# All of w_down's columns by Strassen's algorithm in groups 0 to 6 of a two-layer encoder, with results added on GpSimd

## The chip, the cores and the metric

The kernel runs on one core of one Trainium2 chip. The metric is the device time of one execution in microseconds (us). A core has TensorE (PE, matrix multiply; PEld is its weight load), VectorE (DVE), ScalarE (ACT) and GpSimd (POOL), which run side by side from queues in program order, and SyncE (SP), which issues most transfers. SBUF is the on-chip memory, PSUM the eight banks into which TensorE writes.

## The reference, cut to what matters

Two layers of a bidirectional encoder on 256 tokens of width 2048. The change lies in the last two lines of a layer:

```python
for l in range(DEPTH):
    ...
    x = x + jnp.einsum('bse,ed->bsd', mix, w_o[l])
    h = rmsnorm(x, norm_mlp[l])
    u = jax.nn.relu(jnp.einsum('bsd,df->bsf', h, w_up[l]))
    x = x + jnp.einsum('bsf,fd->bsd', u * u, w_down[l])
return rmsnorm(x, norm_final)
```

Here w_up is 2048 x 8192 and w_down 8192 x 2048, all in 32-bit floats.

## The kernel before, in words

**Steps.** All weight products are cut into steps, one per 128x1024 block of weights (512 KB), kept in one list (`Step`, L465). For each step the program, written out by the loop at the end, does three things ahead of its matmuls: `load` (L964) issues the transfer seven steps ahead on SP's queue; `split` (L978) cuts the weights into a high part `whi` (a cast on ScalarE, L988) and a low part `wlo` (a subtraction on VectorE, L989), two or three steps ahead, into three buffers each; and `prep`, where a step has one, runs five steps ahead. A product is then the sum of high x high, high x low and low x high, so a weight block costs one ScalarE and one VectorE instruction of 1024 columns besides its matmuls.

**The MLP.** The 8192 hidden columns are cut into eight groups of 1024. `up_steps(g)` (L657) has 16 steps, four for each block `q` of 256 hidden columns; the block is evacuated by ScalarE and VectorE (L668 to L676: sum, rectify and scale, square, split). Its result `uT[q]` has a high and a low part. For the Strassen products `sums_of` (L707) forms the four sums S1 to S4 of the left factor (L712 to L714) and splits them (L716, L717). Group g + 1's w_up steps are mixed with group g's w_down steps by the list `order` (L846).

**w_down.** Before, columns 1024 to 2047 of a group are plain steps (`down_steps`, 8 steps of 12 matmuls through `mode_b`, L477), and columns 0 to 1023 are one 2 x 2 Strassen product in Winograd's form (`strassen_steps`, L761): seven products P1 to P7, two steps each (one per half `h` of the rows), six matmuls per step (L802) instead of the plain form's eight products. The right factors are sums of weight blocks, formed by VectorE (L815, L817, L821, L832) in place or into `t2`. Three PSUM banks (`a`, `d`, `b`) carry the products, `a` and `d` accumulating over several of them. After each product its bank is added to or subtracted from x by VectorE (L782, PSUM and SBUF in, SBUF out). Group 7 is plain.

**Buffers.** Raw weights land in `wraw` (five), or for Strassen in `spare0`, `spare1` (B11, one per row half) and `side` (four: B12, B22, B21). `mid` has six buffers of 512 columns, `big` has 24, and the matmul banks are six besides the pair of `score_banks`.

Of the kernel before, what the change touches and what calls it, by code (L numbers as in the profile page):

```python
# [23 lines left out]
P = 128  # L24
# [19 lines left out]
def tile_trunk(ctx: ExitStack, tc: tile.TileContext, x_in, w_in, w_o, w_up, w_down,  # L44
# [459 lines left out]
    def layer_steps(l):  # L504
# [152 lines left out]
        def up_steps(g):  # L657

            out_, evacs = [], []
            for q in range(4 * g, 4 * g + 4):  # L660
                box = {}

                def evac(q=q, box=box):
                    need(("rrow", l))
                    a = mid(F32, 2, 256)
                    for i in range(2):

                        nc.scalar.copy(a[:, i, :], box["b"][i][:, 256:512])  # L668
                        nc.vector.tensor_add(a[:, i, :], a[:, i, :], box["b"][i][:, 0:256])
                    nc.vector.scalar_tensor_tensor(  # L670
                        a, a, 0.0, rrow.rearrange("p (o c) -> p o c", o=1).to_broadcast([P, 2, 256]),
                        op0=ALU.max, op1=ALU.mult)
                    nc.scalar.activation(a, a, AF.Square, bias=zero1[:, 0:1])
                    u = big(F32R, 2, 2, 256)
                    nc.scalar.copy(u[:, 0], a)
                    nc.vector.tensor_sub(u[:, 1], a, f(u[:, 0]))  # L676
                    uT[q] = u
                    if q < 28:
                        sums_of(q, a)
# [27 lines left out]
        def sums_of(q, a):  # L707
# [3 lines left out]
            a11, a21, a12 = v[:, 0, :], v[:, 1, :], v[:, 2, :]  # L711
            nc.vector.tensor_sub(sm[:, 0:2, :], v[:, 0:4:3, :], v[:, 1:2, :].to_broadcast([P, 2, P]))  # L712
            nc.vector.scalar_tensor_tensor(sm[:, 2, :], sm[:, 1, :], -1.0, a11, op0=ALU.mult, op1=ALU.subtract)
# [6 lines left out]
        def down_steps(g, js):  # L720
            out_ = []
            for j in js:
                box = {}
                for k in range(4):
                    def mm(wh, wl, j=j, k=k, box=box):
                        if k == 0:
# [3 lines left out]
                        hts = [uT[4 * g + k]] * 2  # L730
                        mode_b(box["b"], hts, wh, wl, [0, 1], k == 0, k == 3, blocks=(0,) if final else (0, 1),
                               lo_last=g < 7)
# [7 lines left out]
                        if final:  # L740
# [3 lines left out]
                            for c in range(2):  # L744
                                cols = slice(c * 256, c * 256 + 256)
                                for i, (hts, vh, vl) in enumerate(box["w"]):
                                    mode_b([None, tail[c]], hts, vh[:, :, cols], vl[:, :, cols], [0, 1],
# [10 lines left out]
                    out_.append(Step(w_down[l, (g * 4 + j) * 4 + k], 2, 512, None, mm, fourth=g == 7))  # L758
            return out_

        def strassen_steps(g):  # L761
# [5 lines left out]
            raw, t2, box = {}, {}, {}  # L767

            def src(par, j, h):
                return w_down[l, g * 16 + (par * 2 + j) * 2 + h]  # L770

            def left(name, q):

                if name[0] == "A":
                    t, kk = int(name[1]) - 1, int(name[2]) - 1
                    return [uT[q][:, i, kk, t * P:(t + 1) * P] for i in range(2)]
                return [sT[q][:, i, "3124".index(name[1]), :] for i in range(2)]

            def evac(bank, t, j, sign):
                xs = x[:, t, j * 512:(j + 1) * 512]  # L780
                op = nc.vector.tensor_add if sign > 0 else nc.vector.tensor_sub
                op(xs, xs, bank)  # L782


            plan = [("P1", "A11", "a", True, (0, 0, 1)), ("P6", "S2", "a", False, (1, 0, 1)),
                    ("P7", "S3", "d", True, (1, 1, -1)), ("P5", "S1", "a", False, (1, 1, -1)),
                    ("P3", "S4", "a", False, (0, 1, -1)), ("P2", "A12", "b", True, (0, 0, 1)),
                    ("P4", "A22", "d", False, (1, 0, 1))]
            out_ = []
            for name, lf, bk, fresh, dst in plan:  # L790
                for h in range(2):
# [19 lines left out]
                    elif name == "P6":  # L811
                        loads = [(("B12", h), src(0, 1, h), None), (("B22", h), src(1, 1, h), None)]

                        def prep(h=h):
                            nc.vector.tensor_add(raw["B11", h], raw["B11", h], raw["B12", h])  # L815
                            t2[h] = big(F32, 2, 512)
                            nc.vector.tensor_add(t2[h], raw["B22", h], raw["B11", h])  # L817
                        get = lambda h=h: t2[h]
                    elif name == "P7":
                        def prep(h=h):  # L820
                            nc.vector.tensor_add(raw["B12", h], raw["B12", h], raw["B22", h])  # L821
                        get = lambda h=h: raw["B12", h]
# [4 lines left out]
                    elif name == "P2":  # L827
                        loads = [(("B21", h), src(1, 0, h), None)]
                        get = lambda h=h: raw["B21", h]
                    else:  # L830
                        def prep(h=h):
                            nc.vector.tensor_add(t2[h], raw["B21", h], t2[h])  # L832
                        get = lambda h=h: t2[h]
                    stp = Step(None, 2, 512, None, mm, fourth=False, prep=prep, raw=get,
# [5 lines left out]
        for g in range(7):  # L840
            ss = down_steps(g, (2, 3)) + up_steps(g + 1)
            hs = strassen_steps(g)

            order = [0, 0]
            for p_ in range(7):
                order += [1, 0, 1] + ([0, 0] + [0] * (p_ in (1, 3, 5)) if p_ < 6 else [])  # L846
            assert order.count(0) == len(ss) and order.count(1) == len(hs), (order.count(0), order.count(1))
            steps.extend(hs.pop(0) if o else ss.pop(0) for o in order)
        steps.extend(down_steps(7, range(4)))
# [258 lines left out]
def _pack_down(w, g):  # L1108

    plain = [_pack(w[:, j * 512:(j + 1) * 512], 2) for j in range(4)]  # L1110
    if g < 7:
        b = w.reshape(8, P, D)
        plain[0:2] = [np.stack([b[[4 * h + par, 4 * h + par + 2], :, j * 512:(j + 1) * 512].transpose(1, 0, 2).reshape(P, 1024)
                                for j in range(2) for h in range(2)]) for par in range(2)]
    return np.concatenate(plain)
# [59 lines left out]
```

## Time and profile before

| what | value |
| --- | --- |
| time, median of 3 runs | 2020.19 us (2019.79 to 2020.29) |
| profiled execution, its own time | 2019.96 us |
| its span, first to last instruction | 2018.2 us |
| granted TensorE clock, mean | 0.999 |
| mean transfer rate | 189 GB/s, 381.28 MB in all |

Times of single instructions come from the profiled execution. An instruction row names line, engine, operation, output <- inputs, shape and count; then come busy us, mean ns of one, and the idle time of the engine in front of it with what ended it.

### The profile page before, as it was taken

To read this page: it belongs to the slowest core of one execution; us is meant where nothing else is said; L and a number is where in the kernel's file an instruction comes from. 1 tells how busy PE (TensorE), PEld (TensorE's weight loads), DVE (VectorE), ACT (ScalarE), POOL (GpSimd) and SP (SyncE) were. 2 spreads that over 40 slices of the span, in tenths; PEclk is the share of its full clock that TensorE was granted. 3 is DMA by queue.
4 is the path that set the end of the run, shared out by engine and by line. 5 is a ranking of instruction groups with operands and counts; after the bars stand their busy time and mean duration, and the time that the engine had idled before them with its cause. 6 is when DMAs were issued, how large, how long until landed. Compare 5 with 4: busy or idle time off the path is not lost.

```text
span 2018.2 us, 27873 instructions
## 1 busy us (share of the span) xinstructions
PE 2003.0 (99%) x10264; PEld 1707.6 (85%) x10264; DVE 1644.0 (81%) x2095; ACT 1208.2 (60%) x1748; POOL 257.2 (13%) x296
## 2 busy tenths in 40 slices
PE   9999999999999999999999999999999999999998
PEld 7888788888888888888888888888888888888887
DVE  6777977879888898887658789778888888888975
ACT  6667756565555556555656676565655556565554
POOL 0493330000000000000005744200000000000001
PEclk9999999999999999999999999999999999999999
DMA  8655465566565756656656455565665756657554
GB/s 279 197 167 154 165 190 188 175 212 191 184 222 171 223 186 190 213 173 199 188 179 185 156 165 175 180 188 181 194 210 174 231 167 209 203 170 235 165 166 156
DMA packets 108821, 381.28 MB, mean 189 GB/s; under 512 B 12259, under 2 KB 16611, under 8 KB 108684
## 3 DMA queue, kind: packets, MB, share of 16 engines
q1 hardware_dynamic: 108252, 378.41, 59.0%
q8 instruction: 80, 1.31, 0.2%
q10 hardware_dynamic: 432, 1.10, 0.1%
q14 instruction: 57, 0.47, 0.1%
HBM read 377.34 MB, written 2.11 MB: 188 GB/s over the span
## 4 chain that ended last, share of the span: by engine, by line
PE 93%; DVE 3%; ACT 1%; POOL 1%; issue 1%; DMA 1%; SPq 0%; DVEq 0%; POOLq 0%
PE mm L477 40%; PE mm L691 23%; PE mm L696 12%; PE S L802 11%; PE mm L802 2%; PE tr L392 1%; PE tr L219 1%; POOL big L939 1%; DVE wlo L989 1%; PE tr L411 1%; ACT big L372 1%; DVE big L287 1%; PE S L351 1%; PE S L350 1%; DVE big L394 0%
## 5 line engine op out<-in xcount | busy, mean ns | idle before, releaser
L988 ACT CAST whi<-wraw 128x1024 fp32r<-128x1024 f32 (+1 forms) x531 | 556.9, 1051 | 421.9 <-PE mm L691 170.2
L989 DVE TENSOR_TENSOR wlo<-wraw,whi 128x1024 fp32r<-128x1024 f32 (+1 forms) x531 | 655.9, 1237 | 184.7 <-ACT whi L988 181.8
L477 PE MATMUL mm<-whi,big 128*128 128x512 f32 (+1 forms) x2252 | 643.8, 386 | 0.3 <-ACT whi L988 0.3
L691 PE MATMUL mm<-big,whi 128*128 128x512 f32 x2048 | 509.6, 391 | 0.0
L477 PEld LDWEIGHTS mm<-whi,big 128*128 128x128 f32 x2252 | 419.0, 188 | 82.9 <-ACT whi L988 2.3
L691 PEld LDWEIGHTS mm<-big,whi 128*128 128x128 f32 x2048 | 377.4, 188 | 73.7
L477 PE MATMUL mm<-wlo,big 128*128 128x512 f32 (+1 forms) x1126 | 375.7, 385 | 1.0 <-DVE wlo L989 1.0
L696 PEld LDWEIGHTS mm<-big,wlo 128*128 128x128 f32 x2048 | 279.5, 191 | 19.9
L696 PE MATMUL mm<-big,wlo 128*128 128x256 f32 x2048 | 285.7, 283 | 0.0
L477 PEld LDWEIGHTS mm<-wlo,big 128*128 128x128 f32 x1126 | 212.0, 188 | 41.8 <-DVE wlo L989 2.3
L802 PE MATMUL S<-whi,big 128*128 128x512 f32 x672 | 182.3, 393 | 0.0
L477 PE MATMUL mm<-spare,big 128*128 128x512 f32 (+1 forms) x678 | 158.5, 382 | 0.0
L988 ACT CAST whi<-side 128x1024 fp32r<-128x1024 f32 x84 | 88.3, 1051 | 95.5 <-PE mm L691 78.0
L477 PEld LDWEIGHTS mm<-spare,big 128*128 128x128 f32 x678 | 122.3, 188 | 23.1
L802 PEld LDWEIGHTS S<-whi,big 128*128 128x128 f32 x672 | 119.2, 189 | 18.6
L989 DVE TENSOR_TENSOR wlo<-side,whi 128x1024 fp32r<-128x1024 f32 x84 | 102.6, 1222 | 37.2 <-ACT whi L988 36.9
L383 POOL TENSOR_SCALAR big<-big,sm 128x256 f32<-128x256 f32 x128 | 89.4, 716 | 247.0 <-DVE sm L381 208.9
L255 POOL TENSOR_TENSOR sm<-sm,mhalf 128x2 f32<-128x2 f32 (+2 forms) x14 | 13.4, 954 | 793.5 <-DVE sm L250 773.6
L988 ACT CAST whi<-big 128x1024 fp32r<-128x1024 f32 x56 | 58.9, 1052 | 85.3 <-DVE big L817 36.4
L802 PE MATMUL S<-wlo,big 128*128 128x512 f32 x336 | 104.0, 391 | 0.0
L870 POOL TENSOR_TENSOR x<-x,big 128x512 f32<-128x512 f32 x6 | 8.6, 1456 | 669.5 <-ACT mid L877 669.5
L988 ACT CAST whi<-spare 128x1024 fp32r<-128x1024 f32 x56 | 59.0, 1053 | 47.8 <-PE mm L691 27.8
(152 smaller groups left out, 2093.8 us busy)
## 6 DMA issues: line engine op xcount, KB each, us to landing
wraw<-in_w_up_dram SPq DMA_DIRECT2D x256, 512.0 KB, 4.2
wraw<-in_w_down_dram SPq DMA_DIRECT2D x144, 512.0 KB, 3.7
wraw<-in_w_in_dram SPq DMA_DIRECT2D x119, 512.0 KB, 3.8
side<-in_w_down_dram SPq DMA_DIRECT2D x84, 512.0 KB, 4.3
wraw<-in_w_o_dram SPq DMA_DIRECT2D x64, 512.0 KB, 3.9
spare<-in_w_down_dram SPq DMA_DIRECT2D x28, 512.0 KB, 4.3
side<-in_rpb_dram SPq DMA_DIRECT2D x32, 174.8 KB, 5.0
side<-avec SPq DMA_DIRECT2D x8, 384.0 KB, 5.2
```

The costliest lines, as they stand in the source:

```text
L219: tr = nc.tensor.transpose(psv[:, kk, t, :], x[:, t, c0:c0 + P], ident).ins
L287: nc.vector.tensor_sub(kl[rows, par::2, :], z, f(kh[rows, par::2, :]))
L350: nc.tensor.matmul(o, st, u.kh[:, kh, :], start=True, stop=False)
L351: nc.tensor.matmul(o, st, u.kl[:, kh, :], start=False, stop=True)
L372: nc.scalar.activation(p[:, s, :], src[s], AF.Exp, bias=negm[:, s:s + 1], scale=u.rq[:, s:s + 1] if u.kind == "C" else 1.0, accum_out=sums ...
L383: nc.gpsimd.tensor_scalar(p[:, s, :], p[:, s, :], rs[:, s:s + 1], 1.0, op0=ALU.mult, op1=ALU.mult)
L477: return nc.tensor.matmul(banks[t][:, 0:n], a, (wl if part == "hl" else wh)[:, i, :], start=first and i == 0 and part == "hh", stop=last a ...
L691: nc.tensor.matmul(box["b"][fs], wh[:, kk, fs * P:(fs + 1) * P], ht, start=s == 0 and kk == 0, stop=False, skip_group_check=True)
L696: nc.tensor.matmul(box["b"][fs][:, 0:256], wl[:, kk, fs * P:(fs + 1) * P], ht[:, 0:256], start=False, stop=s == 3 and kk == 3, skip_group_ ...
L802: nc.tensor.matmul(o, ops[i][a], w[:, i, :], skip_group_check=True, start=fresh and h == 0 and i == 0 and a == 0 and w is wh, stop=h == 1 ...
L988: act = nc.scalar.copy(h[:, part], w[:, part]).ins
L989: last_lo[0] = nc.vector.tensor_sub(lo[:, part], w[:, part], f(h[:, part])).ins
```

## The change

In groups 0 to 6 both halves of the 2048 columns become Strassen products: `strassen_steps(g, half)` is called twice, `down_steps` only for group 7. Steps per group go from 16 + 8 + 14 to 16 + 28.

- The order of the seven products is now P1, P7, P6, P2, P5, P4, P3. The mixing list has two Strassen steps and one w_up step per product.
- `evac`: ScalarE copies the bank into a `mid` buffer, and GpSimd adds it to or subtracts it from x. VectorE takes no part.
- The right factor of P4, t2 + B21, is no longer a VectorE sum: a transfer issued by GpSimd reads B21 a second time from memory and accumulates into `t2`. B21's own buffer is used for P2 alone.
- The two halves of a block of `u` are stored in swapped order, so that the three blocks used by the Strassen products lie side by side; for blocks below 28 only 384 of the 512 columns are split. `sums_of` forms the same four sums in another order.
- `down_steps` loses the use of `spare` as a fourth pair of split buffers and the option `lo_last`; w_down is packed on the host accordingly.

The diff, cut to its core:

```diff
                     for i in range(2):
-                        nc.scalar.copy(a[:, i, :], box["b"][i][:, 256:512])
-                        nc.vector.tensor_add(a[:, i, :], a[:, i, :], box["b"][i][:, 0:256])
+                        nc.scalar.copy(a[:, 1 - i, :], box["b"][i][:, 256:512])
+                        nc.vector.tensor_add(a[:, 1 - i, :], a[:, 1 - i, :], box["b"][i][:, 0:256])
...
-                    u = big(F32R, 2, 2, 256)
-                    nc.scalar.copy(u[:, 0], a)
-                    nc.vector.tensor_sub(u[:, 1], a, f(u[:, 0]))
+                    u = big(F32R, 2, 512)
+                    n, af = 384 if q < 28 else 512, a.rearrange("p k c -> p (k c)")
+                    nc.scalar.copy(u[:, 0, 0:n], af[:, 0:n])
+                    nc.vector.tensor_sub(u[:, 1, 0:n], af[:, 0:n], f(u[:, 0, 0:n]))
...
-                    out_.append(Step(w_down[l, (g * 4 + j) * 4 + k], 2, 512, None, mm, fourth=g == 7))
+                    out_.append(Step(w_down[l, (g * 4 + j) * 4 + k], 2, 512, None, mm))
...
-        def strassen_steps(g):
+        def strassen_steps(g, half):
...
             def evac(bank, t, j, sign):
-                xs = x[:, t, j * 512:(j + 1) * 512]
-                op = nc.vector.tensor_add if sign > 0 else nc.vector.tensor_sub
-                op(xs, xs, bank)
+                xs = x[:, t, half * 1024 + j * 512:half * 1024 + (j + 1) * 512]
+                c = mid(F32, 512)
+                nc.scalar.copy(c, bank)
+                op = nc.gpsimd.tensor_add if sign > 0 else nc.gpsimd.tensor_sub
+                op(xs, xs, c)
-            plan = [("P1", "A11", "a", True, (0, 0, 1)), ("P6", "S2", "a", False, (1, 0, 1)),
-                    ("P7", "S3", "d", True, (1, 1, -1)), ("P5", "S1", "a", False, (1, 1, -1)),
-                    ("P3", "S4", "a", False, (0, 1, -1)), ("P2", "A12", "b", True, (0, 0, 1)),
-                    ("P4", "A22", "d", False, (1, 0, 1))]
+            plan = [("P1", "A11", "a", True, (0, 0, 1)), ("P7", "S3", "d", True, (1, 1, -1)),
+                    ("P6", "S2", "a", False, (1, 0, 1)), ("P2", "A12", "b", True, (0, 0, 1)),
+                    ("P5", "S1", "a", False, (1, 1, -1)), ("P4", "A22", "d", False, (1, 0, 1)),
+                    ("P3", "S4", "a", False, (0, 1, -1))]
...
+                    elif name == "P7":
+                        loads = [(("B12", h), src(0, 1, h), None), (("B22", h), src(1, 1, h), None)]
+                        def prep(h=h):
+                            nc.vector.tensor_add(raw["B11", h], raw["B11", h], raw["B12", h])
+                            nc.vector.tensor_add(raw["B12", h], raw["B12", h], raw["B22", h])
                     elif name == "P6":
                         def prep(h=h):
-                            nc.vector.tensor_add(raw["B11", h], raw["B11", h], raw["B12", h])
                             t2[h] = big(F32, 2, 512)
                             nc.vector.tensor_add(t2[h], raw["B22", h], raw["B11", h])
...
                     elif name == "P2":
                         loads = [(("B21", h), src(1, 0, h), None)]
+                        def prep(h=h):
+                            nc.gpsimd.dma_start(t2[h], src(1, 0, h).rearrange("p (k n) -> p k n", k=2),
+                                                accum_op=ALU.add)
                     else:
-                        def prep(h=h):
-                            nc.vector.tensor_add(t2[h], raw["B21", h], t2[h])
                         get = lambda h=h: t2[h]
...
-            ss = down_steps(g, (2, 3)) + up_steps(g + 1)
-            hs = strassen_steps(g)
+            ss = up_steps(g + 1)
+            hs = strassen_steps(g, 0) + strassen_steps(g, 1)
             order = [0, 0]
-            for p_ in range(7):
-                order += [1, 0, 1] + ([0, 0] + [0] * (p_ in (1, 3, 5)) if p_ < 6 else [])
+            for p_ in range(14):
+                order += [1, 0, 1] + [0] * (p_ == 6) if p_ < 13 else [1, 1]
```

55 lines of the change are left out of this document (28 added, 27 removed).

## The prediction

> **What bounds the kernel now.** I read the page's first part, then the busy times by stretch, then the chain of waits, to see which engine has no slack in the stage that the change touches.
>
> ```profile
> span 2018.2 us, 27873 instructions
> PE 2003.0 (99%) x10264; PEld 1707.6 (85%) x10264; DVE 1644.0 (81%) x2095; ACT 1208.2 (60%) x1748; POOL 257.2 (13%) x296
> ```
>
> The profiled execution took 2019.96 us, 1.8 us around its span of 2018.2, and stands 0.23 us under the median of 2020.19. I add to 2019.96; a difference under 0.2% (4 us) cannot be told from none here. TensorE (PE) is the bound on average, with VectorE (DVE) behind it. The change touches only the MLP of each layer, where one group of 1024 hidden rows repeats. Two of these groups in the view of busy times by stretch (the five engines in the order PE, weight load, DVE, ACT, POOL):
>
> ```profile
> 452.93:538.42 85.49, 85.49 (x437) 73.17 (x437) 73.67 (x91) 49.14 (x59) 0.00 (x0) 1.00 0.62 197
> 538.42:623.92 85.50, 85.50 (x438) 73.17 (x437) 73.67 (x91) 49.16 (x59) 0.00 (x0) 1.00 0.62 197
> ```
>
> The reader is to see three things: a group takes 85.49 us, TensorE has no gap in it, and VectorE is busy 73.67 us of it, so it has 11.8 us to give. GpSimd (POOL) does nothing at all. There are seven such groups in each of two layers, 14 in all. The chain of waits inside a group is TensorE alone:
>
> ```profile
> 538.42 5.44 PE mm L477 x24
> ...
> 565.62 1.81 PE mm L691 x8
> 567.44 0.95 PE mm L696 x8
> 568.39 1.39 PE S L802 x6
> ```
>
> The 24 matmuls are two plain steps of w_down (2.72 us each), the next two rows one step of w_up (2.76), the last one Strassen step (1.39, of 6 matmuls). A group has 8, 16 and 14 of them.
>
> **TensorE, what goes.** The 8 plain steps go (8 x 2.72 = 21.8 us) and 14 Strassen steps come (14 x 1.39 = 19.5). TensorE's group falls by 2.3 us to 83.2, 32 us over 14 groups. That is all there is to win.
>
> **VectorE, packed price.** It must now be summed, since it had only 11.8 us. Its instructions start before the last one's record ends:
>
> ```profile
> 474.69 1.22 DVE L821 TENSOR_TENSOR side<-side,side 128x1024 f32<-128x1024 f32 x1
> 475.83 0.68 DVE L782 TENSOR_TENSOR x<-x,S 128x512 f32<-128x512 f32 x1
> 476.43 1.22 DVE L989 TENSOR_TENSOR wlo<-wraw,whi 128x1024 fp32r<-128x1024 f32 x1
> ```
>
> From start to start, 128x1024 costs 1.14 us and 128x512 0.60: the duration less 0.08. The groups of instructions of the stretch 538.42 to 623.92 give the kinds and durations (mean ns after the comma; counts are up to one off, as the stretch cuts instructions):
>
> ```profile
> L989 DVE TENSOR_TENSOR wlo<-wraw,whi 128x1024 fp32r<-128x1024 f32 x25 | 30.6, 1222 | 6.4 <-ACT whi L988 6.2
> L782 DVE TENSOR_TENSOR x<-x,S 128x512 f32<-128x512 f32 x6 | 4.1, 679 | 0.0
> L739 DVE TENSOR_TENSOR x<-x,mm 128x512 f32<-128x512 f32 x4 | 2.6, 681 | 0.0
> L815 DVE TENSOR_TENSOR spare<-spare,side 128x1024 f32<-128x1024 f32 x2 | 2.4, 1219 | 0.0
> L669 DVE TENSOR_TENSOR mid<-mid,mm 128x256 f32<-128x256 f32 x9 | 3.4, 414 | 0.0
> L670 DVE SCALAR_TENSOR_TENSOR mid<-mid,rrow 128x512 f32<-128x512 f32 x4 | 2.7, 683 | 0.0
> L676 DVE TENSOR_TENSOR big<-mid,big 128x512 fp32r<-128x512 f32 x4 | 2.8, 688 | 0.1
> L717 DVE TENSOR_TENSOR big<-mid,big 128x512 fp32r<-128x512 f32 x4 | 2.7, 684 | 0.0
> L712 DVE TENSOR_TENSOR mid<-mid 128x256 f32<-128x256 f32 x4 | 1.7, 419 | 0.0
> L714 DVE SCALAR_TENSOR_TENSOR mid<-mid,mid 128x128 f32<-128x128 f32 x4 | 1.1, 287 | 0.0
> ```
>
> Before, by the code: 38 splits (8 + 16 + 14 steps) x 1.14 = 43.3; 8 weight sums (the kind of L815) x 1.14 = 9.1; 11 results added to x (7 of L782, 4 of L739) x 0.60 = 6.6; four blocks of w_up at 2 x 0.33 + 0.60 + 0.61 + 0.60 + 0.34 + 2 x 0.21 = 3.23 each, 12.9. Together 71.9, near the 73.67 recorded, so the price list holds.
>
> After:
> - 16 + 28 = 44 splits: 50.2 us (six more).
> - Weight sums: six per half group, for P7 two and for P6 one per row half; P4's go to the accumulating transfer. 12 x 1.14 = 13.7.
> - The 11 results leave VectorE: 0.
> - Blocks of w_up: L676 shrinks from 512 to 384 columns (an estimate of 0.12 less): 3.11 x 4 = 12.4. The other reordering of blocks and rows (swapped halves, other sum order) has the same instructions and costs nothing.
>
> That is 76.3 us of VectorE under 83.2 of TensorE. Alone, it would fit.
>
> **GpSimd's 14 adds.** Each result is now copied by ScalarE and added to x by GpSimd, 128x512 with both inputs in SBUF. The trace has exactly this instruction at the end, on the same tensor x, beside VectorE splits (first the record of line L870 with its shortest, median and longest ns, then both engines in order of time, start and us):
>
> ```profile
> L870 POOL TENSOR_TENSOR x<-x,big x6: 1282/1457/1625, 1979.3 to 2002.6; 128x512 f32<-128x512 f32 x6
> ...
> 1979.26 2.87 POOL L870 TENSOR_TENSOR x<-x,big 128x512 f32<-128x512 f32 x2 [653.46 <-ACT mid L877]
> ...
> 1978.50 1.23 DVE L989 TENSOR_TENSOR spare<-wraw,spare 128x1024 fp32r<-128x1024 f32 x1 [0.30 <-ACT spare L988]
> 1981.26 1.95 DVE L989 TENSOR_TENSOR wlo<-wraw,whi 128x1024 fp32r<-128x1024 f32 x1 [1.54 <-ACT whi L988]
> 1983.98 1.23 DVE L989 TENSOR_TENSOR wlo<-wraw,whi 128x1024 fp32r<-128x1024 f32 x1 [0.77 <-ACT whi L988]
> ```
>
> This is the row on which the forecast turns. The undisturbed split takes 1.23 us, the one that began while GpSimd was adding 1.95. And GpSimd waits in turn: its add takes 1.28 alone, 1.63 for the first, which began while the split of 1978.50 ran. They take turns; neither slows to half. The price in a packed row: the split in front ends at 1979.73, the first add at 1979.26 + 1.63 = 1980.89, so 1.16 after it; the second add ends at 1982.13 and the split behind it at 1983.21, 1.08 after. Split to split over one add is then 2.24 against 1.14: an add costs VectorE 1.10 us. It happens also in the middle of the kernel, on other operands:
>
> ```profile
> 125.94 1.30 POOL L317 TENSOR_TENSOR big<-big,ctab_q 128x512 f32<-128x512 f32 x1
> ...
> 126.34 1.98 DVE L989 TENSOR_TENSOR spare<-wraw,spare 128x1024 fp32r<-128x1024 f32 x1 [0.44 <-ACT spare L988]
> ```
>
> The Trainium skill, SBUF — State Buffer, section "Who interferes with whom", says that a VectorE instruction with two SBUF inputs and a GpSimd instruction that reads SBUF exclude each other for the whole instruction. By that rule an add would cost its full 1.28, the group 2.5 us more, and the time would come to 2164; the trace shows 1.10, as the start and end of an add overlap with its neighbours.
>
> All of VectorE's work has two SBUF inputs except L669 (one input in a matmul bank), 2.6 us of 76.3. So 14 x 1.10 = 15.4 joins VectorE's 76.3: 91.7 us, less about 0.5 for adds that fall beside L669 (3% of 15.4). This is over TensorE's 83.2: the bound changes engine.
>
> **Waits in a saturated VectorE.** VectorE's queue is in order, so whatever waits in it now lies on the path; behind a waiting sum stand the splits that TensorE needs.
>
> ```profile
> L832 DVE TENSOR_TENSOR big<-side,big 128x1024 f32<-128x1024 f32 x28 | 34.3, 1225 | 29.3 <-DMA side<-in_w_down_dram 29.3
> side<-in_w_down_dram SPq DMA_DIRECT2D x84, 512.0 KB, 4.3
> ```
>
> The sum L832 waited 29.3/28 = 1.05 us for its load each time, hidden until now. It goes, but P7's first sums are in its place: prepared five steps ahead, on loads issued seven ahead, into the four side buffers, two of which B22 holds until P3, the last product. With four such sums per group the cost lies between 0 and 4.2 us; I take 2.1.
>
> **ScalarE, queues, transfer.** A bank-to-SBUF cast and the split's cast:
>
> ```profile
> L393 ACT CAST big<-tr 128x512 fp32r<-128x512 f32 x64 | 34.9, 589 | 1.5 <-PE tr L392 1.0
> L988 ACT CAST whi<-wraw 128x1024 fp32r<-128x1024 f32 x24 | 25.3, 1053 | 19.4 <-PE mm L691 9.8 <-PE mm L477 4.6 <-PE S L802 3.0
> ```
>
> 49.2 + 14 x 0.59 + 6 x 1.05 = 63.8 us in 93: nothing, cover 29 us. The bank is free again after the copy, and a product's bank is next used 5 us later (2.8 between halves): nothing. GpSimd has 14 x 1.6 = 23 us of adds. Its four accumulating issues per group wait for P6's split (a VectorE split per row half); behind a waiting issue stand only adds to x, which nobody in the group reads. No transfer of before accumulates. It has the time from P6's split to P4's, nine steps at 93/44 = 2.1 us, 19 us; even at twice a load's 4.3 us it is hidden, so nothing. A gain is excluded, since the sum that it replaces is already counted as gone. A Trainium skill figure for a GpSimd-issued transfer (DMA: Bandwidth & Descriptors, "Anatomy of one DMA — SWDGE (gpsimd) path": 2.0 us plus bytes over 436 GB/s) gives an estimate of 3.2 us for a plain 0.5 MB; no run here shows it. SP's queue keeps its 32 loads per group; the last group (g = 7) loses the spare pair as a fourth buffer, in a stage where no Strassen step or add stands beside VectorE's work: nothing.
>
> **Sum.** 91.7 - 0.5 + 2.1 = 93.3 us per group against 85.5: +7.8, 14 times +109: 2019.96 + 109 = 2129 us.
>
> **Rivals.**
> - *TensorE stays the bound.* GpSimd's adds would have to fall into VectorE's gaps: 83.2 us are left less 76.3 = 6.9 us, room for 6 adds of the 14. It decides by the price of an add: under 6.9/14 = 0.49 us the kernel gets faster, 2020 - 32 = 1988 us. For it: VectorE alone fits. Against: 1.95 instead of 1.23, twice seen. Chance 0.06.
> - *Half hidden.* Adds find the waits of VectorE for ScalarE and cost some 0.6 us: 76.3 + 8.4 = 84.7 and some waits, 85 to 86 us: 2020 us. The 6.4 us of such waits per group in the L989 row speak for it, but they exist because VectorE had time. Chance 0.05.
> - *The accumulating transfer is late.* Should it take over 19 us, P4's split waits in VectorE's queue. Each us late costs 4 x 14 = 56 us: 2 us late gives 2129 + 112 = 2241. For it: nothing in the trace shows its pace. Against: it is four times a load. Chance 0.09.
> - That the change does not do what it says (the matmuls not falling by 12 x 14 = 168) has no sign in the diff; I give it nothing.
>
> **How the numbers follow.** The forecast, VectorE and GpSimd in turn, has 0.80. Its ends: three of the 14 adds hidden and no load waits, 88.4 us, +41, 2061; an add at 1.28 in full with 4.2 us of waits, 98.4 us, +181, 2201. Both ends together are unlikely; 2070 to 2185 keeps 0.8 of all cases, the fast, half hidden and late ones outside. Faster 0.06 (first rival), same 0.02 (the middle of the second), slower 0.92.
>
> **What would show it.** Right: TensorE with gaps before its matmuls released by wlo (L989 of before), some 10% of the MLP; the split's mean duration in the MLP up from 1.22 to about 1.4 or 1.5, GpSimd's adds at 1.3 to 2.4; a group's period of 91 to 96 us. Wrong: a period of 83 us with splits at 1.22 (first rival), or VectorE idle before P4's split, released by a transfer (third).

## The result, and the profile after

The median after is 2196.23 us (2194.83 to 2197.74, four runs) against 2020.15 (2019.79 to 2020.29) for the kernel before beside it: a ratio of 1.0872 (1.0853 to 1.0891), 176 us slower. The direction was forecast, the size was not: the time lies 67 us above the 2129 forecast and 11 us above the upper end of the range.

The first part of the page of the kernel after, whose profiled execution took 2194.83 us:

```profile
span 2193.0 us, 28703 instructions
PE 2054.9 (94%) x10096; PEld 1683.3 (77%) x10096; DVE 1878.2 (86%) x2081; ACT 1360.9 (62%) x2028; POOL 660.8 (30%) x548
```

TensorE's matmuls fell by 168, from 10264 to 10096, as the diff says, yet TensorE is no longer full. Two neighbouring groups in the view of busy times by stretch, each from one instruction of a w_up block (L670) to the same one a group later:

```profile
576.64:675.84 99.20, 89.23 (x425) 71.08 (x425) 90.68 (x89) 60.05 (x78) 27.86 (x19) 0.98 0.64 191
675.84:775.03 99.19, 89.19 (x425) 71.02 (x425) 90.67 (x89) 60.00 (x78) 27.83 (x19) 0.98 0.65 191
```

A group takes 99.2 us where 93.3 were forecast. TensorE (first) idles 10 us of it. But VectorE (third), which was to be saturated, also idles, 99.20 - 90.68 = 8.5 us. No engine is full: something makes them wait for one another. The groups of instructions of the first stretch:

```profile
L785 POOL TENSOR_TENSOR x<-x,mid 128x512 f32<-128x512 f32 x15 | 26.3, 1750 | 60.2 <-ACT mid L783 60.2
L999 DVE TENSOR_TENSOR wlo<-wraw,whi 128x1024 fp32r<-128x1024 f32 x16 | 21.5, 1344 | 1.7 <-ACT whi L998 1.6
L999 DVE TENSOR_TENSOR wlo<-side,whi 128x1024 fp32r<-128x1024 f32 x13 | 15.8, 1219 | 3.7 <-ACT whi L998 3.7
L999 DVE TENSOR_TENSOR wlo<-spare,whi 128x1024 fp32r<-128x1024 f32 x8 | 11.9, 1491 | 0.0
L819 DVE TENSOR_TENSOR spare<-spare,side 128x1024 f32<-128x1024 f32 x4 | 7.1, 1766 | 0.0
L719 DVE TENSOR_TENSOR big<-mid,big 128x512 fp32r<-128x512 f32 x4 | 2.8, 693 | 2.8 <-ACT big L718 2.8
L836 POOL DMA_DIRECT2D big<-in_w_down_dram x4 | 3.5, 872 | 17.2 <-DVE wlo L999 17.2
```

The exclusion by GpSimd's adds is there: splits of 1344 and 1491 ns on average and weight sums of 1766 instead of 1220. VectorE's idle time, 1.7 + 3.7 + 2.8 of the 8.5 us, ends in every row with a cast on ScalarE (L998, L718), which was to have 29 us to spare. The accumulating transfers (L836) wait for P6's split as foreseen and delay nobody.

So what does ScalarE wait for? The chain of waits, at the end of a group:

```profile
656.02 0.94 PE S L805 x4
656.96 0.02 issue
656.99 1.06 ACT whi L998
658.04 0.04 issue
658.09 2.13 PE mm L693 x8
660.21 0.02 issue
660.24 1.06 ACT whi L998
661.29 0.04 issue
661.34 2.12 PE mm L693 x8
```

TensorE and ScalarE alternate without overlap: matmuls, a cast, the next matmuls, the next cast. That happens when a cast has to wait for the buffer that the matmuls before it free. There are three. ScalarE's and then TensorE's timeline (start, us) show who holds the other two:

```profile
652.33 0.57 ACT L783 COPY mid<-S 128x512 f32<-128x512 f32 x1
654.18 2.00 ACT L998 CAST whi<-side 128x1024 fp32r<-128x1024 f32 x2 [1.29 <-PE S L805]
...
656.99 1.05 ACT L998 CAST whi<-wraw 128x1024 fp32r<-128x1024 f32 x1 [0.26 <-PE S L805]
660.24 1.05 ACT L998 CAST whi<-wraw 128x1024 fp32r<-128x1024 f32 x1 [2.20 <-PE mm L693]
...
662.36 0.58 ACT L783 COPY mid<-S 128x512 f32<-128x512 f32 x1
```

```profile
658.09 2.11 PE L693 MATMUL mm<-big,whi 128*128 128x512 f32 x8 [0.68 <-ACT whi L998]
...
661.34 2.12 PE L693 MATMUL mm<-big,whi 128*128 128x512 f32 x8 [0.19 <-ACT whi L998]
...
663.77 1.08 PE L805 MATMUL S<-whi,big 128*128 128x512 f32 x4
```

P3's two weight blocks (`side`) are cast from 654.18 to 656.18, and the bank that P3 goes on adding to has been copied since 652.90. Yet P3's matmuls start at 663.77, behind those of two w_up steps that were cast after it, at 656.99 and 660.24. What P3 does come after is the copy of P4 (L783, 662.36 to 662.94), which lies in the other bank, `d`. That copy stands in ScalarE's queue behind the cast of 660.24, which waits for the third buffer. For 7.6 us (656.18 to 663.77) two of the three `whi` buffers are full and unused, and the w_up steps pass one by one through the third. The order is fixed in TensorE's queue, which the scheduler writes when the program is built; the trace does not show why it puts a w_up step ahead of a Strassen step. The theory, which the experiments test, is that it does so where it reckons that the Strassen step will still be waiting. Comparing the order of the casts with that of the first matmuls of each step, 14 of the 44 steps of a group in the middle of a layer are overtaken in this way.

ScalarE has a second wait in such a group, its longest one:

```profile
ACT whi L998 <- DVE side L820: 16.7, 4, 5.2
```

The cast of P7's block needs VectorE's sum (L820), and the casts behind it wait too: at 625.24 TensorE had waited 2.32 us for a w_up block cast behind such a wait. This wait is still 8.8 us a group in e20 and 6.4 in e19 below, where VectorE or TensorE is full all the same.

### The profile page after: what moved, and what is told of

Read it like the earlier page. It is cut to its first block, busy times and chain, and to the rows that moved or that the text cites. A ratio compares the mean times of both kernels' runs of the same rounds, so it can differ in the third digit from the quotient of the medians.

```text
span 2193.0 us, 28703 instructions
## 1 busy us (share of the span) xinstructions
PE 2054.9 (94%) x10096; PEld 1683.3 (77%) x10096; DVE 1878.2 (86%) x2081; ACT 1360.9 (62%) x2028; POOL 660.8 (30%) x548
## 4 chain that ended last, share of the span: by engine, by line
PE 65%; DVE 20%; issue 8%; ACT 5%; DMA 2%; POOL 1%; DVEq 0%; SPq 0%; ACTq 0%; POOLq 0%
PE mm L477 23%; PE mm L693 15%; PE S L805 14%; DVE wlo L999 10%; PE mm L698 7%; DVE spare L819 4%; ACT whi L998 4%; DVE side L820 3%; PE mm L805 2%; PE tr L392 1%; DVE mid L669 1%; PE tr L219 1%; POOL big L949 1%; PE tr L411 0%; ACT big L372 0%
## 5 line engine op out<-in xcount | busy, mean ns | idle before, releaser
L785 POOL TENSOR_TENSOR x<-x,mid 128x512 f32<-128x512 f32 x196 | 355.8, 1815 | 836.0 <-ACT mid L783 836.0
L998 ACT CAST whi<-wraw 128x1024 fp32r<-128x1024 f32 (+1 forms) x419 | 437.7, 1047 | 257.7 <-PE mm L693 111.7
L477 PE MATMUL mm<-whi,big 128*128 128x512 f32 (+1 forms) x1356 | 422.4, 384 | 1.9 <-ACT whi L998 1.9
L805 PE MATMUL S<-whi,big 128*128 128x512 f32 x1344 | 387.5, 408 | 11.0 <-ACT whi L998 8.3
L998 ACT CAST whi<-side 128x1024 fp32r<-128x1024 f32 x168 | 174.9, 1049 | 315.1 <-DVE side L820 222.0
L805 PEld LDWEIGHTS S<-whi,big 128*128 128x128 f32 x1344 | 246.1, 194 | 75.1 <-ACT mid L783 21.1
L477 PEld LDWEIGHTS mm<-whi,big 128*128 128x128 f32 x1356 | 250.4, 188 | 50.7 <-ACT whi L998 4.7
L477 PE MATMUL mm<-wlo,big 128*128 128x512 f32 (+1 forms) x678 | 255.7, 381 | 1.0 <-DVE wlo L999 1.0
L999 DVE TENSOR_TENSOR wlo<-spare,whi 128x1024 fp32r<-128x1024 f32 x112 | 162.6, 1452 | 4.3 <-ACT whi L998 4.3
L805 PEld LDWEIGHTS S<-wlo,big 128*128 128x128 f32 x672 | 130.9, 196 | 34.9 <-DVE wlo L999 5.2
L999 DVE TENSOR_TENSOR wlo<-big,whi 128x1024 fp32r<-128x1024 f32 x112 | 140.5, 1254 | 3.8 <-ACT whi L998 1.2
```

Of the source, the lines that this page charges most:

```text
L477: return nc.tensor.matmul(banks[t][:, 0:n], a, (wl if part == "hl" else wh)[:, i, :], start=first and i == 0 and part == "hh", stop=last a ...
L785: op(xs, xs, c)
L805: nc.tensor.matmul(o, ops[i][a], w[:, i, :], skip_group_check=True, start=fresh and h == 0 and i == 0 and a == 0 and w is wh, stop=h == 1 ...
L998: act = nc.scalar.copy(h[:, part], w[:, part]).ins
L999: last_lo[0] = nc.vector.tensor_sub(lo[:, part], w[:, part], f(h[:, part])).ins
```

## The experiments

The theory of the forecast was that the exclusion alone (VectorE and GpSimd in turn) sets the time. The first four runs take it apart; the others look for the second cause. Beside each median stands its ratio to the kernel before on the same chip. The diffs are cut to their core.

**What the adds cost.** Three edits of `evac`: VectorE adds straight from the bank, as before the change; the copy alone; the copy and three GpSimd writes that read nothing.

```diff
# e1: no copy, no GpSimd
-                c = mid(F32, 512)
-                nc.scalar.copy(c, bank)
-                op = nc.gpsimd.tensor_add if sign > 0 else nc.gpsimd.tensor_sub
-                op(xs, xs, c)
+                op = nc.vector.tensor_add if sign > 0 else nc.vector.tensor_sub
+                op(xs, xs, bank)
# e2: the copy stays
-                op = nc.gpsimd.tensor_add if sign > 0 else nc.gpsimd.tensor_sub
-                op(xs, xs, c)
# e3: as e2, and
+                for _ in range(3):
+                    nc.gpsimd.memset(c, 0.0)
```

e1: 

> One part undone: the 14 results of a group go back to VectorE, which adds the bank to x as before; ScalarE's copies and GpSimd's adds are gone, all else is as changed. Lock theory (VectorE loses 13.0 us per group of 99.2 to GpSimd's adds, by the lengthened instructions of the changed profile): the splits fall back to 1.22 us, VectorE needs 77.7 + 14 x 0.60 = 86.1 us, and if its 8.5 us of waits stay, a group takes 94.6 and the time is about 2130; if the waits shrink with the lock, down to 2030. Clumping theory (the weight sums of P7 and P6 stand close together, two or three buffers of lead cannot carry them, and elsewhere VectorE idles): the waits stay, nearer 2130 than 2030. Transfer theory (the accumulating transfer or ScalarE's queue holds things up): little gained, above 2150.

e2: 

> Leaves out the additions of groups 0 to 6 to x; ScalarE's copies stay, GpSimd keeps only the four accumulating transfers of a group. Lock theory: 13.0 us per group go, 99.2 to 86 at most, 182 us of the time: 2014 or less, with splits at 1.22; and since VectorE then needs 77.7 under TensorE's 83, the waits should shrink too, to about 1990. Transfer theory: the copies and transfers are still there, so the time stays above 2150. Clumping theory alone (without the lock being worth its 13 us): 2080 or more.

e3: 

> Leaves out the additions, and gives GpSimd three memsets of the 128x512 copy in place of each, which write SBUF and read nothing. Lock on reading (only GpSimd instructions that read SBUF exclude VectorE's second input): splits at 1.22 and the time of the kernel with no additions at all, within 5 us. Rival, any GpSimd instruction on SBUF excludes VectorE, or GpSimd's being busy slows it: splits well over 1.3 in the groups and 2100 or more.

Measured: e1 2088.29 us (1.0337; 1.0319 to 1.0354), e2 2118.87 (1.0489; 1.0473 to 1.0504), e3 2119.18 (1.0492; 1.0476 to 1.0507). GpSimd's adds cost 77 us (2196 to 2119), and GpSimd has to read for that: e3's 588 writes of 0.53 us each cost nothing, and its splits stay at 1222 ns:

```profile
L785 POOL MEMSET mid<- 128x512 f32 x588 | 310.8, 529 | 822.9 <-ACT mid L783 800.4
L999 DVE TENSOR_TENSOR wlo<-spare,whi 128x1024 fp32r<-128x1024 f32 x112 | 136.9, 1222 | 23.6 <-ACT whi L998 21.3
```

But e2, with no add at all, is still 99 us slower than before. One group of it:

```profile
600.00:693.60 93.60, 87.41 (x425) 69.74 (x425) 78.66 (x89) 60.39 (x79) 3.49 (x4) 1.00 0.67 203
```

93.6 us, with VectorE idle for 14.9 of it and TensorE for 6. There is a second cause without GpSimd. And e1, which adds 14 x 0.6 us to VectorE, is faster than e2, which takes that work away: the copy by ScalarE costs more than the addition on VectorE. Yet e1 too is 68 us slower than before: its group takes 90.3 us with TensorE busy for 85.8 and VectorE for 85.7, so neither is full there.

**Adds by a transfer.** The add becomes an accumulating transfer from `mid` into x, so that no arithmetic of GpSimd reads SBUF:

```diff
-                nc.scalar.copy(c, bank)
-                op = nc.gpsimd.tensor_add if sign > 0 else nc.gpsimd.tensor_sub
-                op(xs, xs, c)
+                nc.scalar.activation(c, bank, AF.Copy, scale=float(sign))
+                nc.gpsimd.dma_start(xs, c, accum_op=ALU.add)
```

e4: 

> Complete computation: ScalarE copies the bank with the sign as a scale, and GpSimd issues an accumulating transfer from the copy to x in place of its add. Lock theory: the transfers read through other ways, VectorE needs 77.7 us per group again and TensorE 83 bounds it: 1990 to 2030, below the kernel of before if the clumps cost under 2 us per group. Rival, the transfers (14 x 256 KB more per group, 10 us each with the copy's buffer held) run late or their issue excludes VectorE as the adds do: 2060 or more, with ScalarE waiting for mid buffers.

Measured: 2129.5 us (1.0541; 1.0525 to 1.0557), a group of 93.6 us as in e2, splits at 1.22. The exclusion is gone, the second cause stays.

**The transfer that replaces P4's sum.** Undone, with the sum back on VectorE:

```diff
                     elif name == "P2":
                         loads = [(("B21", h), src(1, 0, h), None)]
-                        def prep(h=h):
...
-                            nc.gpsimd.dma_start(t2[h], src(1, 0, h).rearrange("p (k n) -> p k n", k=2),
-                                                accum_op=ALU.add)
...
                     else:
+                        def prep(h=h):
...
+                            nc.vector.tensor_add(t2[h], raw["B21", h], t2[h])
                         get = lambda h=h: t2[h]
```

e5: 

> One part undone: P4's right factor t2 + B21 is again a VectorE sum, four per group, and the accumulating transfer goes; GpSimd's additions stay. If the transfer is hidden as the prediction had it, the four sums (4 x 1.14 = 4.6 us per group) come on top: about 99.2 + 4 = 103, 2240 to 2265. If the transfer itself holds the products up, it comes out at 2196 or below.

Measured: 2221.06 us (1.0994; 1.0976 to 1.1013). The transfer saves 25 us; it is not the second cause. Four sums of 1.14 us would be 4.6 us a group, but a group grew by 2.1 (99.2 to 101.3): part of them must have fallen into VectorE's gaps.

**The mixing of the steps.** The new list needs 28 Strassen splits between 16 w_up steps. The theory here is that VectorE's work clumps around the weight sums. This edit puts more w_up steps beside the products around which the sums fall:

```diff
+            ups = (2, 2, 1, 0, 1, 0, 2, 2, 2, 1, 0, 1, 0, 0)
             for p_ in range(14):
-                order += [1, 0, 1] + [0] * (p_ == 6) if p_ < 13 else [1, 1]
+                order += [[1, 1], [1, 0, 1], [1, 0, 1, 0]][ups[p_]]
```

e6: 

> The changed kernel complete, with the same steps in another order: two w_up steps each beside P1 and P7, around which the weight sums fall, one beside P6, P5 and P3 or none. Clumping theory: VectorE's waits shrink and the group falls from 99.2 to 93 to 96 us, 2110 to 2150. Buffer theory: more places with Strassen steps in a row, the same or worse, 2190 to 2230.

Measured: 2278.88 us (1.1282; 1.1265 to 1.1298), groups of 104 to 108 us. The theory that VectorE's work clumps gets no support, but the edit brings in another wait and so is no clean test. Only 3 of 44 steps are overtaken in e6, and of its 31.2 us of waits from 600 to 810 us TensorE spends 21.1 on ScalarE's copies, all before P4:

```profile
PE S L805 <- ACT mid L783: 21.1, 4, 6.1
```

So overtaking alone does not set the time. What speaks against clumping is e20 below, where VectorE is full with the sums in their old places.

**The copies, and the buffers.** e10 leaves copies and adds out. e8 gives the kernel after a fourth pair of split buffers (paid with two of the 24 `big`) and lets the splits run one step further ahead; e9 does that to e4, e13 to the kernel before.

```diff
# e10
-                c = mid(F32, 512)
-                nc.scalar.copy(c, bank)
-                op = nc.gpsimd.tensor_add if sign > 0 else nc.gpsimd.tensor_sub
-                op(xs, xs, c)
+                pass
# e8, e9, e13
-        return dp.tile([P, *shape], dt, tag="big", bufs=24, name=nm("big"))
+        return dp.tile([P, *shape], dt, tag="big", bufs=22, name=nm("big"))
-            h = wp.tile([P, s.kk, s.n], F32R, tag="whi", bufs=3, name=nm("whi"))
-            lo = wp.tile([P, s.kk, s.n], F32R, tag="wlo", bufs=3, name=nm("wlo"))
+            h = wp.tile([P, s.kk, s.n], F32R, tag="whi", bufs=4, name=nm("whi"))
+            lo = wp.tile([P, s.kk, s.n], F32R, tag="wlo", bufs=4, name=nm("wlo"))
-        while ns < min(len(steps), i + LOOK_SPLIT + (not s.fourth)):
+        while ns < min(len(steps), i + LOOK_SPLIT + 2 * (not s.fourth)):
```

e10: 

> Leaves out both the additions of groups 0 to 6 and ScalarE's copies of the banks. Queue theory (ScalarE's copies stand in front of casts in its in-order queue): the 93.6 us per group of the kernel without additions falls to 84 to 87, 1985 to 2030. Buffer theory: three buffers are still three; 90 us or more, 2070 or more.

e8: 

> The changed kernel complete, with four buffers each for the high and low parts (paid with 22 instead of 24 of the big buffers) and splits one step further ahead in the MLP. Buffer theory (with three buffers, the chain from a freed buffer over cast 1.05 and subtraction 1.22 to the matmul is about 2.6 us, and two Strassen steps in a row last only 2.75): VectorE's waits of 8.5 us per group shrink to 1 to 3, a group takes 91 to 94 us, 2080 to 2125. Queue theory (casts stand behind a copy, or behind the cast of P7 that waits for VectorE's sum, whatever the buffers): above 2160.

e9: 

> Complete: the additions by accumulating transfers as in the kernel with 2129.5 us, and four buffers and the longer lead. Buffer theory: VectorE's 15 us of waits per group fall below 8, a group takes 84 to 87 us with TensorE 83 as its floor: 1995 to 2040. Queue theory: still 2110 or more.

e13: 

> The kernel of before with four buffers, the longer lead and 22 big buffers. TensorE had no gaps in its groups (85.49 us), so buffers can give nothing: 2018 to 2022. If it is slower, the two big buffers taken away cost in the attention stages, and that much of the other kernels' times is theirs; if it is faster than 2010, the gain of the complete kernel at 2009.9 was the buffers' and not Strassen's.

Measured: e10 2001.23 us (0.9907; 0.9890 to 0.9923), e8 2106.11 (1.0426; 1.0410 to 1.0441), e9 2009.93 (0.9951; 0.9936 to 0.9966), e13 2019.87 (0.9998; 0.9989 to 1.0008). One group of e10 and one of e9:

```profile
600.00:684.10 84.10, 83.63 (x426) 70.76 (x426) 77.39 (x89) 54.41 (x65) 3.49 (x4) 1.00 0.73 225
```

```profile
600.00:683.90 83.90, 83.90 (x426) 70.39 (x425) 77.20 (x90) 61.04 (x78) 15.74 (x18) 1.00 0.94 271
```

Without the copies TensorE is full again, though ScalarE had been busy for only 60 of 93.6 us: it is not the copy's 0.58 us that costs, but its place between two products. In e10 one step of 44 is overtaken in TensorE's queue, in e1 11, in e2, e4 and after 14. A fourth buffer cures it as well, while 14 steps are still overtaken in e8 and e9: with two buffers held by overtaken steps, two are left for the others. e9 is 10 us faster than the kernel before; e13 shows that the buffers alone bring the kernel before nothing.

**Where the copy stands on ScalarE.** Perhaps the copy waits for the product's last matmul and blocks the next split's cast behind it. e11 writes the copy one step later in the program, e14 does so with four buffers, e16 ties it behind the next step's cast, e18 does this to the kernel after.

```diff
# e11, e14 (on e4, e9)
-                            evac(o, *dst)
+                            pend.append(lambda: evac(o, *dst))
# one step later, after the splits
+        while pend:
+            pend.pop(0)()
# e16 (on e4), e18 (on after)
+        while pend:
+            with tc.issue_after(last_act[0]):
+                pend.pop(0)()
```

e11: 

> Complete; the kernel with additions by accumulating transfers and three buffers (2129.5 us, 93.6 us per group), with one thing moved: ScalarE's copy of a finished bank is queued one step later, behind the next step's cast instead of in front of it. Order theory (the copy lengthens the chain from a freed buffer over cast and subtraction to the matmul only because it stands in front of the cast): 84 to 88 us per group, 1995 to 2050. Work theory (ScalarE's 8.1 us of copies per group cost by their mere number, wherever they stand): unchanged, 2110 to 2130.

e14: 

> Complete; additions by accumulating transfers, four buffers and the late copy together. TensorE is already without gaps in the groups with four buffers alone (83.9 us), so nothing more is to be had there: 2000 to 2012, the same as with four buffers within 0.3%. If the copy's place still mattered, below 2000.

e16: 

> Complete; the same kernel (2129.5 us) with ScalarE's copy of a finished bank tied behind the cast of the step that follows, so that its place in ScalarE's queue really changes, which the attempt before did not achieve. Copy theory: 84 to 88 us per group, 1995 to 2050. TensorE-order theory: 92 or more unless the order of TensorE's matmuls changes with it.

e18: 

> The changed kernel with GpSimd's additions, three buffers, with the copies tied behind the following step's cast. Copy theory: 91 to 94 us per group, 2080 to 2125. TensorE-order theory: 2170 or more.

Measured: e11 2128.73 us (1.0537; 1.0522 to 1.0553), e14 2008.19 (0.9940; 0.9925 to 0.9955), e16 2136.52 (1.0574; 1.0558 to 1.0590), e18 2203.82 (1.0907; 1.0890 to 1.0923). e11 and e14 decide nothing: the copies stand in ScalarE's order where they stood in e4 and, but for four of 196, in e9, and e14 cannot be told from e9 (groups of 83.9 us in both). e16 and e18 moved two of the 14 copies of a group in the middle of a layer behind a cast, left the other twelve in place, and lost 7 and 8 us. That speaks against a copy ahead of a cast as the cause, but for two copies only; e19 below settles it.

**TensorE's queue in program order.** Each MLP step's first matmul is tied behind the last matmul of the step before it, so that no step is overtaken; e15 on e4, e17 on the kernel after (`last_mm` is the last matmul written so far).

```diff
-        s.mm(hi_t.pop(i), lo_t.pop(i))
+        with tc.issue_after(last_mm[0]) if not s.fourth and last_mm[0] is not None else nullcontext():
+            s.mm(hi_t.pop(i), lo_t.pop(i))
```

e15: 

> Complete; additions by accumulating transfers, three buffers (2129.5 us), with one thing fixed: each MLP step's matmuls stand in TensorE's queue behind all of the step before, where so far a w_up step's matmuls were cut in two by Strassen steps. TensorE-order theory (a step that is cut in two holds its high and low buffer through the steps in between, so three buffers do not suffice): 84 to 88 us per group, 1995 to 2050. Copy theory (the copy in front of the cast): 92 us or more, 2100 or more.

e17: 

> The changed kernel with GpSimd's additions, three buffers, with TensorE's order fixed in the same way. The lock stays (VectorE and the lock need 77.7 + 13.0 = 90.7 us): if order was the rest, 91 to 94 us per group and 2080 to 2125, as with four buffers (2106). If not, 2180 or more.

Measured: e15 2398.67 us (1.1882; 1.1862 to 1.1902), e17 2409.64 (1.1928; 1.1910 to 1.1946), in e15 groups of 113 to 116 us. My expectation fell with them: without overtaking, TensorE stands in the wait that the overtaking had filled. The waits of e15 from 600 to 800 us (total, times, longest):

```profile
PEld S L805 <- ACT mid L784: 40.8, 14, 4.8
PE S L805 <- ACT mid L784: 34.8, 14, 4.3
```

Both rows are the same 14 waits, the first as the weight loads see them, so they must not be added. The 34.8 us are all of TensorE's idle time in these 200 us (it is busy for 165.2): it waits for ScalarE's copies. Which copies? Here, from ScalarE's and TensorE's timelines together (start, us), are P1's copy, P7's two steps and P7's copy, and the first step of P6:

```profile
606.46 0.60 ACT L784 ACTIVATE mid<-S 128x512 f32<-128x512 f32 x1 [1.24 <-PE S L805]
607.11 1.20 PE L805 MATMUL S<-whi,big 128*128 128x512 f32 x4 [0.69 <-ACT mid L784]
...
611.37 1.09 PE L805 MATMUL S<-whi,big 128*128 128x512 f32 x4
...
616.61 0.59 ACT L784 ACTIVATE mid<-S 128x512 f32<-128x512 f32 x1
617.26 2.08 PE L805 MATMUL S<-whi,big 128*128 128x512 f32 x4 [4.34 <-ACT mid L784]
```

P6 (617.26) goes on adding in bank `a`, which was copied by 607.06; it waits until P7's copy from bank `d` ends at 617.20. P7 (607.11), which starts anew in `d`, waits likewise for P1's copy from `a`. The two banks are one tile of the program (`score_banks`), and the wait holds for the pair: in after and in every run above that copies banks, no product in it starts before the copy of the product ahead of it in the pair has ended (earliest 0.05 us after), though P7, P6, P4 and P3 have had their own bank free for 4.7 us or more. In e1 the same holds for VectorE's additions. Over all of e15 these waits come before P3 (106 us), P6 (99), P4 (35) and P7 (19), each of which follows directly on a product in the other bank.

**A bank for each product.** This removes the wait itself. Each product starts in a bank and tile of its own, taken in turn from the six matmul banks, so no product has to wait for the copy of the one ahead of it. The two kernels leave out the adding of one product to the next, and so x receives each product alone; e19 on e4, e20 on the kernel after.

```diff
-                        if (name, h) == ("P1", 0):
-                            pair = score_banks().rearrange("p (b i) n -> p b (i n)", i=2)
-                            box["a"], box["d"] = pair[:, 0], pair[:, 1]
-                        if (name, h) == ("P2", 0):
-                            box["b"] = mm_bank()
-                        o = box[bk]
+                        if h == 0:
+                            box[name] = mm_bank()
+                        o = box[name]
...
-                                                 start=fresh and h == 0 and i == 0 and a == 0 and w is wh,
+                                                 start=h == 0 and i == 0 and a == 0 and w is wh,
```

e19: 

> Leaves out that products accumulate on one another: each of the 14 products of a group gets a fresh bank of the six and is added to x alone, by an accumulating transfer as in the kernel with 2129.5 us; copies, steps, splits and three buffers are the same. Bank theory (P6, P5, P3 and P4 must wait until ScalarE's queue, held up behind casts and squares, has copied the bank that they go on adding to; TensorE's queue has w_up steps put in front of them, and so three buffers are held too long): 84 to 87 us per group, 1995 to 2040, with hardly a step overtaken. If it is the copies' mere work in ScalarE's queue: still 92 to 94, 2110 to 2130.

e20: 

> Leaves out the same accumulation, in the changed kernel with GpSimd's additions and three buffers. Bank theory: the lock alone remains, 91 to 94 us per group, 2085 to 2125, as with four buffers (2106). Work theory: 97 or more, 2165 to 2196.

Measured: e19 1996.68 us (0.9882; 0.9866 to 0.9899), e20 2099.27 (1.0391; 1.0375 to 1.0406), with no step overtaken in either; P6 now starts up to 8.9 us before P7's copy ends (e20). All the copies, the adds to x, the split buffers and the matmuls are still there. One group of e19 and one of e20:

```profile
600.00:683.60 83.60, 83.30 (x426) 70.67 (x425) 77.39 (x89) 60.50 (x79) 15.82 (x18) 1.00 0.94 271
```

```profile
600.00:691.10 91.10, 85.99 (x426) 69.92 (x425) 90.80 (x89) 60.59 (x79) 46.69 (x18) 1.00 0.69 208
```

In e20 VectorE is full (90.80 of 91.10) and a group takes what the forecast had for VectorE and GpSimd in turn, 91.2 us. In e19, without GpSimd's adds, TensorE is full. The two causes are thus apart: from after, own banks take 97 us (2196.2 to 2099.3); transfers in place of the adds then take 103 more (to 1996.7); and that stands 23 us under the kernel before, which is the gain of the Strassen products. Making `a` and `d` two tiles of one bank each and keeping the adding was not run; by e15 it should remove the same waits but the one of P1, which follows P3 in the same bank.

## Why the prediction was right or wrong

- **TensorE, 83.2 us.** Right: 83.6 to 84.1 us where nothing else binds (e19, e9, e10). Of the 32 us to win, 23 appear in e19 and 10 in e9.
- **VectorE's packed work, 76.3 us.** Nearly: 77.4 in e19.
- **GpSimd's adds, 1.10 us each.** The mechanism was right; e20 against e19 gives (90.80 - 77.39)/14 = 0.96 us an add. The Trainium skill's rule (SBUF — State Buffer, "Who interferes with whom") of exclusion for a whole instruction is borne out in kind, by e3 too, in which GpSimd writes and does not read; its size here is 0.96 of an add's 1.28.
- **Waits in VectorE's queue, 2.1 us, for P7's loads.** Wrong in place and size: 8.5 us, for ScalarE's casts.
- **Accumulating transfer.** Right: nothing is late. It lands in 7.3 us (median) of the 19 that it has, not the 3.2 estimated from the Trainium skill's figure (DMA: Bandwidth & Descriptors, "Anatomy of one DMA — SWDGE (gpsimd) path") for a plain one.
- **ScalarE and the banks.** This is the step that failed: "The bank is free again after the copy, and a product's bank is next used 5 us later (2.8 between halves): nothing". It priced ScalarE by its busy time. The 5 us hold for the single bank, but the program waits for the pair: P7, P6, P4 and P3 may not start before the copy of the product just ahead, and ScalarE's queue, which is in order, makes that copy late. P4's last matmul ends at 657.41 in after and its copy at 662.94; in e15, where nothing overtakes, TensorE stands up to 4.6 us before such a product. In the kernel before, VectorE added straight from the bank and TensorE had no gap. With the copy in between, w_up steps stand ahead of these products in TensorE's queue; overtaken steps then hold two of the three pairs of buffers, the rest run as a chain of cast, subtraction and matmul through one, and the copy itself stands behind a cast that waits for that buffer. That is 97 us (after against e20). Why the scheduler chose this order is inferred from e15, e19 and e20, not seen. Part of the two causes hides behind one another: from after, own banks alone take 97 us, transfers in place of the adds alone 67 (e4), both 200 (e19).

The sum forecast for a group was 76.3 + 14.9 + 2.1 = 93.3. Measured in after: 90.7 of VectorE's work, of which 77.4 to 78.7 is what it takes without adds (e19, packed, and e2, with gaps) and 12.0 to 13.3 the adds; and 8.5 of waits. The 5.9 us more would be 83 us over 14 groups; the time is 67 above. The forecast counted 14 whole groups; what those at a layer's start and end make of the difference was not followed up.

None of the three rivals holds. The direction was right for the reason given, but without the exclusion the kernel would still have been slower than before (e4; that its 2129.5 us are the forecast's number is chance), for a reason that had been set at nothing.

Open: whether ScalarE's and TensorE's queues, both ordered by hand, could do with three buffers what four do; that was not tried. Why e9 wins 10 us and not the 14 x 1.6 = 22 of its groups is settled only in part: at the end of layer 1 a load of w_down holds up the chain of waits for 10.75 us there, and TensorE stood for 5.7.

## What to carry to other kernels

An engine's spare time says nothing about whether a new instruction on it is free: ask who may not start before that instruction ends, and where a matmul may not start before another engine has copied a bank, that engine's queue belongs to TensorE's path. Check which copy the program really waits for: here a tile of two banks made each product wait for the copy of the other bank. When no engine is full, look for steps in TensorE's queue whose order differs from that of their casts, and count how many buffers those hold. GpSimd additions that read SBUF beside a nearly full VectorE cost it three quarters of their duration here (0.96 of 1.28 us); an accumulating transfer does not (e4, e9), and with one buffer more it made this change worth having.

## What the runs showed of the hardware

**GpSimd can be starved.** An add whose shortest record in the kernel before is 1.28 us takes much longer beside a VectorE that has few gaps (after) or none (e20). The adds in after and in e20 (line record: shortest, median and longest ns):

```profile
L785 POOL TENSOR_TENSOR x<-x,mid x196: 1333/1796/7409, 379.1 to 2144.1; 128x512 f32<-128x512 f32 x196
```

```profile
L785 POOL TENSOR_TENSOR x<-x,mid x196: 1297/1788/15268, 379.3 to 2048.1; 128x512 f32<-128x512 f32 x196
```

In e20 the mean is 3.0 us and one took 15.3. During that one VectorE ran fourteen instructions with two SBUF inputs one after another without a gap (1775.55 to 1789.11 us); the add ended 1.24 us after VectorE had begun two L669, which take one input from a bank. Whoever reads such a result soon would have to count on it; here nobody does within the group.

**Accumulating transfers.** From memory to SBUF 512 KB land 7.3 us after issue in after (median); from SBUF to SBUF 256 KB take as long, 7.3 in e9. Their issue took GpSimd 0.87 us and did not lengthen VectorE's splits (1.22 us in e9).

```profile
big<-in_w_down_dram POOLq DMA_DIRECT2D x56, 512.0 KB, 7.3
```

```profile
x<-mid POOLq DMA_DIRECT2D x196, 256.0 KB, 7.3
```

**The granted clock.** In e15's group TensorE is busy 95.84 of 116 us for the same matmuls, at a granted clock of 0.88 where e9's group has 1.00:

```profile
600.00:716.00 116.00, 95.84 (x431) 78.19 (x430) 80.76 (x90) 62.81 (x79) 15.74 (x18) 0.88 0.74 195
```

A TensorE with gaps thus lost twice in that run, by its waits and by slower matmuls; what sets the clock was not measured.
